# First weights of an encoder loaded and split by halves between x's chunks, and a final norm that multiplies from PSUM

## The chip, the core and the metric

The kernel runs on one core of a Trainium2 chip. The metric is the device time of one execution in microseconds; before and after are compared by the median of several runs. The core has five engines that work at the same time and wait for each other by semaphores: TensorE (PE) multiplies matrices, VectorE (DVE), ScalarE (ACT) and GpSimd (POOL) do elementwise work, and SyncE (SP) issues the transfers between HBM and the on-chip memory. [...]

## The reference, cut to what matters

Two layers of an encoder over 512 positions of width 1024, in fp32. The change touches the first projection and the last norm.

```python
for l in range(2):
    x = x + hybrid_mixer(rms_norm(x, norm_mix[l]), w_in[l], ...)   # neighbourhood and grouped-query attention
    x = x + memory_cross_attention(rms_norm(x, norm_mem_q[l]), ...)
    x = x + conv_ffn(rms_norm(x, norm_ffn[l]), w_up[l], ..., w_down[l])
return rms_norm(x, norm_final)

def rms_norm(x, g):
    return x * rsqrt(mean(x * x, axis=-1) + 1e-6) * g
```

The first thing that is multiplied is `rms_norm(x, norm_mix[0]) @ w_in[0]`, a product of 512x1024 by 1024x2304.

## The kernel before, in words

x is held transposed, as eight tiles `xT[0..7]` of 128 features (partitions) by 512 positions. To keep nearly fp32 accuracy at the speed of a shorter format, every operand is split into two parts, `hi` (rounded) and `lo` (the remainder), and a product is three matmuls: hi x hi, hi x lo, lo x hi (`mm3`, `gemm_T`). The gain of a norm is multiplied into x when x is split (`Norm.operand`: ScalarE makes hi with the gain as its scale, VectorE makes lo). The factor 1/rms isn't known yet at that time; it is multiplied into the result of the projection later. It comes from the squares of x (`Norm.square`), which are added up over the chunks, summed over the partitions by matmuls with a vector of ones (`Norm.stat`), raised to the power -0.5 on GpSimd, and spread over all partitions by matmuls (`Norm.spread`, `row_rep`), which end in a PSUM tile `tr`. ScalarE copies that tile to `rep` in SBUF, and later products read `rep`.

**The weights.** All weight tiles of the program stand in one list, `plan`, in order of use. `emit_raw` issues the load of the next entry on SP's queue; `emit_split` casts it to hi on ScalarE and subtracts on VectorE or GpSimd to get lo. A raw weight tile has two buffers (`N_RAW`), so that a load waits until the split before the last has freed its buffer; `eng` "x" takes the tile from another pool. Before the main program the kernel writes out its first loads by hand: a small piece of the parameters (the gains of the first norm), then `xT[0]`, the first weights (two halves of 256 KB), `xT[1]`, the second weights (512 KB in one transfer), `xT[2]`, `xT[3]`, the third weights (512 KB), `xT[4]` to `xT[7]`, all on SP's queue. A chunk of x is 256 KB too. The matching splits follow in the same order, on ScalarE in the order written (`ACT_IN_ORDER`); on VectorE they are left to the scheduler. Ten matmuls on an identity (`N_WARM`) run on TensorE while the first loads are on their way.

**The first projection** (`project_first`) multiplies three weight tiles (units 0, 1, 2) in an order by pieces, so that TensorE starts on the first chunks of x: chunks 0 and 1 of unit 0, of unit 1, then chunks 2 and 3 of both, chunks 0 to 3 of unit 2, and so on up to chunk 7; 72 matmuls of 128x128 by 128x512. The norm's statistic follows.

**The last stage** (`down_last`) computes the last part of the feed-forward block in two halves of 256 positions, eight rows of 128 features each. When a row is done, VectorE adds it to `xT`, and ScalarE squares it for the final norm. For rows 2 and 5 GpSimd then multiplies `xT` by the final gain `gfin` (`scale`). `finish` spreads 1/rms and makes the output: rows 2 and 5 as `xT * rep` on GpSimd, the others on VectorE as `(xT * gfin) * rep`, two inputs and a scalar in one instruction, all from SBUF. Four transfers per half carry it out, two rows each. The first half's `finish` runs in the middle of the second half's matmuls, the second half's stands at the very end of the program.

The order of a queue is that of the program where it says so (`InOrder`: TensorE, SP, and ScalarE at the start), and that of the tile scheduler elsewhere; `behind(n)` lowers the priority of what is written in it.

Of the kernel before, what the change touches and what calls it, by code (L numbers as in the profile page):

```python
# [11 lines left out]
F32R = mybir.dt.float32r  # L12
AF = mybir.ActivationFunctionType
# [5 lines left out]
P = 128  # L19
# [29 lines left out]
GQA_FILL = [2300] * 16 + [3000] * 4  # L49
MEM_FILL = [1, 1, 1, 2, 1, 0, 0, 2, 0, 1, 2]  # L50
MEM_STEPS = [0, 0, 1, 0, 1, 1, 1, 1, 1, 1, 1] + [0] * 9
W_BEHIND, N_RAW, N_W, AHEAD, AHEAD_HELD, N_WARM, N_LATE, N_FIRST = 45, 2, 4, 2, 5, 10, 4, 3


class InOrder:
# [117 lines left out]
def encoder_kernel(ctx: ExitStack, tc: tile.TileContext, t: dict, out: bass.AP):  # L173
# [58 lines left out]
    plan, raws, ready = [], [], []  # L232
    done = [0]

    def emit_raw():
        key, loads, nk, ncol, eng = plan[len(raws)]
        if eng[1:] == "x":
            raw = rtile((nk, ncol), F32)
        else:
            raw = wpool.tile([P, nk, ncol], F32, tag="raw", name=nm("raw"), bufs=N_RAW)  # L240
        for dst, src in loads:
            SP.dma_start(dst(raw), src)
        raws.append(raw)

    def emit_split(act=ACT, cuts=2):
        n = len(ready)
        key, loads, nk, ncol, eng = plan[n]
        raw = raws[n]
        raws[n] = None
        if key[0] in ("up", "down", "memq", "memo"):  # L250
            cuts = 1
        if eng[1:] == "r":
            hi, lo = rtile((nk, ncol)), rtile((nk, ncol))
        else:
            hi = wpool.tile([P, nk, ncol], F32R, tag="hi", name=nm("hi"))
            lo = wpool.tile([P, nk, ncol], F32R, tag="lo", name=nm("lo"))
        with behind(W_BEHIND if done[0] and key[0] not in ("up", "down") else 0):
            for i in range(cuts):
                k = slice(nk * i // cuts, nk * (i + 1) // cuts)
                act.copy(hi[:, k], raw[:, k])  # L260
                (POOL if eng[0] == "P" else DVE).tensor_sub(lo[:, k], raw[:, k], f(hi)[:, k])  # L261
        ready.append((hi, lo))

    def get_w(key, ahead=AHEAD):
        n = done[0]
        assert plan[n][0] == key, (plan[n][0], key)
        ahead = n + 1 + ahead
        while ahead < min(len(plan), n + 1 + AHEAD_HELD) and plan[ahead][4][1:] == "r":
            ahead += 1
        while len(ready) < min(len(plan), ahead):  # L270
            while len(raws) < min(len(plan), len(ready) + N_RAW):
                emit_raw()
            emit_split()
        while len(raws) < min(len(plan), len(ready) + N_RAW):
            emit_raw()
        done[0] += 1
        w = ready[n]
        ready[n] = None
        return w

    def cols(key, w, k0, nk, c0, ncol, eng="P"):
        src = w[k0 * P : (k0 + nk) * P, c0 : c0 + ncol].rearrange("(k p) c -> p k c", p=P)
        if plan:
            loads = [(lambda r: r, src)]
        else:
# [70 lines left out]
    ones = cpool.tile([P, 1], F32, name="ones")  # L356
    nc.vector.memset(ones, 1.0)
    ACT_IN_ORDER.copy(small(1), ones)
    SP.dma_start(par[:, 0, 0:8], t["par"][:, 0, 0:8])
    for c in range(KC):  # L360
        if c in (1, 2, 4):
            emit_raw()
        SP.dma_start(xT[c], t["xT"][c * P : (c + 1) * P, :])
    qkg = cpool.tile([P, DEPTH, 2], F32, name="qkg")
    gfin = cpool.tile([P, KC], F32, name="gfin")

# [25 lines left out]
    def row_rep(rstd, n, tag, bufs):  # L392

        pr = ps_t()
        for b in range(n):
            PE.matmul(pr[:, b * P : (b + 1) * P], rstd[:, b : b + 1].to_broadcast([P, P]), ident,
                      start=True, stop=True)
        rep = tpool.tile([P, n * P], F32, tag=tag, name=nm(tag), bufs=bufs)
        ACT.copy(rep, pr[:, : n * P])
        return rep  # L400

    class Norm:

# [12 lines left out]
            ACT.copy(xT[c], pm)  # L416
            self.square(c, src=pm)

        def operand(self, c, act=ACT, src=None):
# [3 lines left out]
            act.activation(hi, src, AF.Copy, scale=g)  # L423
            DVE.scalar_tensor_tensor(lo, src, g, f(hi), op0=ALU.mult, op1=ALU.subtract)

        def square(self, c, act=ACT, eng=None, src=None):
            sq = tmp((self.n,))
# [21 lines left out]
            self.rstd = rsqrt(pv[:, 0:nb], nb, 1.0 / D)  # L449

        def spread(self):
            self.rep = row_rep(self.rstd, self.n // P, "rep", 1)

    def split_psum(hi, lo, ps, scale=None):
        if scale is None:
# [100 lines left out]
    for l in range(DEPTH):  # L556
# [615 lines left out]
        def down_last(g):  # L1172

            j0, nj = GROUPS[g]
            ops = [acts.pop(j) for j in range(j0, j0 + nj)]
            ws = []

            def scale(half, m):
                xc = xT[m][:, 256 * half : 256 * half + 256]
                POOL.tensor_scalar(xc, xc, gfin[:, m : m + 1], 1.0, op0=ALU.mult, op1=ALU.mult)  # L1180

            def finish(norm):
                norm.spread()
                y = [rtile((4, 256), F32) for _ in range(2)]
                for k in range(KC):
                    yk, xk = y[k // 4][:, k % 4], xT[k][:, norm.cols]
                    if k in scaled:
                        POOL.tensor_mul(yk, xk, norm.rep)
                    else:
                        DVE.scalar_tensor_tensor(yk, xk, gfin[:, k : k + 1], norm.rep, op0=ALU.mult, op1=ALU.mult)  # L1190
# [4 lines left out]
            norms, scaled = [], (2, 5)  # L1195
            for half in range(2):
                cs = slice(256 * half, 256 * half + 256)
                hops = [(hi[:, cs], lo[:, cs]) for hi, lo in ops]
                norms.append(Norm(cols=cs))
                rows = []  # L1200
                for m in range(KC):
                    if half == 0:
                        ws.append(get_w(("down", g, m)))
                    rows.append(ps_mm()[:, :256])
                    late = half == 0 and m < N_LATE
                    gemm_T(rows[m], ws[m], hops, range(nj - 1 if late else nj), 0, nj - 1)
                    for i in [m] if not late else range(N_LATE) if m == N_LATE - 1 else []:
                        if late:
                            gemm_T(rows[i], ws[i], hops, [nj - 1], 0, nj - 1)
                        DVE.tensor_add(xT[i][:, cs], xT[i][:, cs], rows[i])  # L1210
# [106 lines left out]
```

## Time and profile before

| | us |
|---|---|
| median of 3 runs | 1401.05 |
| lowest, highest | 1397.9, 1404.61 |
| the profiled execution | 1401.19 |
| its span in the profile | 1399.2 |

In the rows of the profile, a time is in us from the start of the span unless ns is given. PE is TensorE's matmuls, PEld its weight loads. A row of the timeline gives start, length, engine, line of the kernel, operation, output and inputs with their shapes, and in brackets how long the engine was idle before and what ended that. A cast is the making of hi, `lo<-raw,hi` that of lo. A line L63 is the helper that keeps an engine in program order, L76 the one that issues matmuls, so such rows are told apart by their tiles. The chain of waits is followed back from the last instruction: it names at each time the piece of work on which the end depended.

### The profile page before, as it was taken

The numbers are of one execution on the slowest core, as the hardware profiler recorded it, in microseconds if no ns is written. First come the engines' busy times: TensorE is split into PE (matmuls) and PEld (weight loads), VectorE is DVE, ScalarE is ACT, GpSimd is POOL, SyncE is SP. The second block draws the span as 40 slices with busy tenths as digits, with TensorE's granted clock in tenths as the row PEclk, the third lists the DMA queues.
The fourth block names the chain that finished last, engine by engine and source line by source line (L and its number), as shares of the span: only waits on it lengthen the run. The fifth ranks groups of instructions, "written<-read, shape, count | busy, mean of one in ns | idle before, by whom it ended". The sixth has DMA issues, their size and how long they took to land.

```text
span 1399.2 us, 19213 instructions
## 1 busy us (share of the span) xinstructions
PE 1358.8 (97%) x7092; PEld 1158.8 (83%) x7092; DVE 835.1 (60%) x1421; ACT 702.8 (50%) x1308; POOL 722.9 (52%) x541
## 2 busy tenths in 40 slices
PE   9999899989999999999999989999999999999997
PEld 7897789878888888888888878897788888888897
DVE  5666766363687178358446557744638833861874
ACT  6676577655443144234556656765554423432441
POOL 2458776635544444444635677756264444444452
PEclk9999999999999999999999999999999999999998
DMA  7653312312333333332356523223133333333321
GB/s 210 181 149 95 89 46 71 111 61 61 94 102 103 93 91 96 100 102 84 118 148 167 135 65 95 70 70 103 46 90 102 95 94 102 89 92 106 100 82 60
DMA packets 218173, 138.83 MB, mean 99 GB/s; under 512 B 5984, under 2 KB 211040, under 8 KB 218080
## 3 DMA queue, kind: packets, MB, share of 16 engines
q1 hardware_dynamic: 218080, 137.60, 34.5%
q8 instruction: 56, 0.92, 0.3%
q14 instruction: 37, 0.30, 0.1%
HBM read 125.00 MB, written 2.10 MB: 91 GB/s over the span
## 4 chain that ended last, share of the span: by engine, by line
PE 88%; DVE 4%; ACT 3%; issue 2%; POOL 1%; DMA 1%; SPq 0%; DVEq 0%; ACTq 0%; POOLq 0%
PE mm L76 80%; PE sc L76 3%; PE tr L63 3%; PE tr L76 1%; ACT hi L260 1%; DVE r L457 1%; DMA raw<-in_w_down 1%; POOL lo L261 0%; POOL r L261 0%; DVE xg L457 0%; DMA raw<-in_w_in 0%; DVE s L859 0%; ACT t L800 0%; ACT t L799 0%; DVE t L801 0%
## 5 line engine op out<-in xcount | busy, mean ns | idle before, releaser
L261 POOL TENSOR_TENSOR lo<-raw,hi 128x1024 fp32r<-128x1024 f32 (+2 forms) x268 | 499.6, 1876 | 507.9 <-ACT hi L260 476.3
L76 PE MATMUL mm<-xg,hi 128*128 128x512 f32 x1984 | 617.7, 393 | 4.3 <-DVE t L801 2.9
L76 PEld LDWEIGHTS mm<-xg,hi 128*128 128x128 f32 x1984 | 369.9, 189 | 80.1 <-DVE t L801 3.3
L260 ACT CAST hi<-raw 128x512 fp32r<-128x512 f32 (+2 forms) x276 | 224.5, 836 | 347.0 <-PE mm L76 288.4
L76 PE MATMUL mm<-xg,lo 128*128 128x512 f32 x992 | 387.7, 391 | 0.0
L76 PE MATMUL mm<-r,hi 128*128 128x512 f32 (+1 forms) x1160 | 336.1, 374 | 2.5 <-DVE r L457 2.0
L76 PEld LDWEIGHTS mm<-r,hi 128*128 128x128 f32 x1160 | 210.3, 189 | 41.2 <-DVE r L457 2.8
L1141 DVE SCALAR_TENSOR_TENSOR t<-t,par,t 128x7 f32<-128x7 f32 (+1 forms) x352 | 201.9, 642 | 34.0 <-ACT t L1134 34.0
L76 PEld LDWEIGHTS mm<-xg,lo 128*128 128x128 f32 x992 | 187.1, 189 | 40.3 <-DVE lo L261 0.7
L76 PE MATMUL mm<-r,lo 128*128 128x512 f32 (+1 forms) x580 | 216.1, 373 | 0.0
L76 PEld LDWEIGHTS mm<-r,lo 128*128 128x128 f32 x580 | 109.3, 188 | 19.2
L1126 DVE TENSOR_TENSOR t<-mm,rep 128x512 f32<-128x512 f32 x88 | 60.2, 688 | 78.6 <-PE mm L76 62.1
L463 POOL TENSOR_SCALAR t<-t,s 128x512 f32<-128x512 f32 (+1 forms) x112 | 66.3, 607 | 75.2 <-DVE s L710 38.2
L1143 ACT ACTIVATE t<-t 128x512 f32<-128x512 f32 x44 | 27.9, 633 | 134.7 <-DVE t L1141 134.7
L1147 DVE TENSOR_TENSOR r<-t,r 128x512 fp32r<-128x512 f32 x44 | 90.5, 2056 | 7.3 <-ACT r L1146 4.3
L1170 DVE TENSOR_TENSOR xT<-xT,mm 128x512 f32<-128x512 f32 x32 | 21.9, 686 | 106.8 <-PE mm L76 106.8
L76 PE MATMUL sc<-r,r 128*128 128x256 f32 (+1 forms) x352 | 73.2, 339 | 4.4 <-DVE r L457 1.8
L63 PE MATMUL tr<-ident,t 128*128 128x128 f32 x456 | 62.8, 274 | 11.8 <-DVE r L457 3.8
L63 PEld LDWEIGHTS tr<-ident,t 128*128 128x128 f32 x456 | 52.4, 140 | 20.4 <-issue 7.9
L1134 ACT ACTIVATE t<-t,par 128x512 f32<-128x512 f32 x88 | 66.9, 807 | 3.3 <-DVE t L1126 3.3
L76 PE MATMUL mm<-r,r 128*128 128x256 f32 (+1 forms) x428 | 62.5, 297 | 0.1
L76 PEld LDWEIGHTS sc<-r,r 128*128 128x128 f32 x352 | 51.8, 191 | 10.6 <-ACT r L456 3.0
(134 smaller groups left out, 1538.9 us busy)
## 6 DMA issues: line engine op xcount, KB each, us to landing
raw<-in_w_up SPq DMA_DIRECT2D x88, 512.0 KB, 3.9
raw<-in_w_in SPq DMA_DIRECT2D x34, 512.0 KB, 4.7
raw<-in_w_down SPq DMA_DIRECT2D x32, 448.0 KB, 3.8
raw<-in_w_mem_kv SPq DMA_DIRECT2D x16, 512.0 KB, 4.1
raw<-in_w_down SPq DMA_DIRECT2D x16, 512.0 KB, 4.2
r<-in_bias SPq DMA_DIRECT2D x16, 384.0 KB, 5.9
r<-r SPq DMA_DIRECT2D x22, 256.0 KB, 5.5
raw<-in_w_out SPq DMA_DIRECT2D x8, 512.0 KB, 3.7
```

The source lines that it names most:

```text
L63: return lambda *a, **k: self.tc.keep_in_program_order(op(*a, **k))
L76: return self.tc.keep_in_program_order(self.engine.matmul(out, lhsT, rhs, **k))
L260: act.copy(hi[:, k], raw[:, k])
L261: (POOL if eng[0] == "P" else DVE).tensor_sub(lo[:, k], raw[:, k], f(hi)[:, k])
L457: DVE.tensor_sub(lo, ps, f(hi))
L463: eng.tensor_scalar(e, e, sums[:, col : col + 1], 1.0, op0=ALU.mult, op1=ALU.mult)
L1126: DVE.tensor_mul(u, us[side], ffn.rep)
L1134: ACT.activation(cc, u, AF.Identity, bias=par[:, l, CB + ch : CB + ch + 1], scale=w[1])
L1141: DVE.scalar_tensor_tensor(cc[:, dst], u[:, src], wi, cc[:, dst], op0=ALU.mult, op1=ALU.add)
L1143: ACT.activation(cs[0], cs[0], AF.Silu)
L1147: DVE.tensor_sub(acts[j][1], cs[0], f(acts[j][0]))
L1170: DVE.tensor_add(xT[m], xT[m], pm)
```

## The change

It has two parts.

1. **The start.** The first three weight tiles are each loaded in two halves of four chunks, 256 KB each, and the halves stand among the chunks of x in a list, `FIRST`: x0, first half of the weights 0 (`w00`), x1, `w10`, x2, x3, `w20`, x4, `w01`, x5, `w11`, `w21`, x6, x7. Loads and splits both follow it. The first parameters are issued on ScalarE's queue in place of SP's. The casts stay on ScalarE, but for that of `w00`, which goes to VectorE; VectorE's own work at the start is now in the order written as well (`DVE_IN_ORDER`), and stands as cast of `w00`, lo of x0, lo of `w00`, lo of x1, and so on. In `project_first` the first piece multiplies the four products with the first weights' hi ahead of the two with its lo. The warm-up has eight matmuls in place of ten.
2. **The end.** `scale` covers all eight rows and runs on ScalarE, with lowered priority, so that `xT` holds x times the final gain before 1/rms is known. The products of `finish` on VectorE become `xT * tr`: two inputs, of which the second is the spread norm where TensorE left it, in PSUM. GpSimd still makes rows 2 and 5 from the copy `rep`, which ScalarE still makes. In the built program VectorE's first product of a half waits for that copy.

```diff
-W_BEHIND, N_RAW, N_W, AHEAD, AHEAD_HELD, N_WARM, N_LATE, N_FIRST = 45, 2, 4, 2, 5, 10, 4, 3
+W_BEHIND, N_RAW, N_W, AHEAD, AHEAD_HELD, N_WARM, N_LATE, N_FIRST = 45, 2, 4, 2, 5, 8, 4, 3
...
     def cols(key, w, k0, nk, c0, ncol, eng="P"):
-        if plan:
+        if len(plan) >= 3:
             loads = [(lambda r: r, src)]
         else:
             h = nk // 2
...
-    SP.dma_start(par[:, 0, 0:8], t["par"][:, 0, 0:8])
-    for c in range(KC):
-        if c in (1, 2, 4):
-            emit_raw()
-        SP.dma_start(xT[c], t["xT"][c * P : (c + 1) * P, :])
+    FIRST = ["x0", "w00", "x1", "w10", "x2", "x3", "w20", "x4", "w01", "x5", "w11", "w21", "x6", "x7"]
+    nc.scalar.dma_start(par[:, 0, 0:8], t["par"][:, 0, 0:8])
+    first_loads = []
+    for n in FIRST:
+        c = int(n[1])
+        if n[0] == "x":
+            SP.dma_start(xT[c], t["xT"][c * P : (c + 1) * P, :])
+            continue
+        if c == len(first_loads):
+            first_loads.append(raw_tile())
+        raw, loads = first_loads[c]
+        dst, src = loads[int(n[2])]
+        SP.dma_start(dst(raw), src)
...
     nn = Norm(G_MIX, 0)
-    for c in range(KC):
-        nn.operand(c, ACT_IN_ORDER)
-        if c in (0, 1, 3):
-            emit_split(ACT_IN_ORDER)
+    DVE_IN_ORDER = InOrder(tc, nc.vector)
+    for n in FIRST:
+        c = int(n[1])
+        if n[0] == "x":
+            nn.operand(c, ACT_IN_ORDER, dve=DVE_IN_ORDER, hi_only=c == 0)
+            continue
...
+        raw, (hi, lo) = raws[c], ready[c]
+        k = slice(4 * int(n[2]), 4 * int(n[2]) + 4)
+        if n == "w00":
+            DVE_IN_ORDER.tensor_copy(hi[:, k], raw[:, k])
+            nn.operand(0, lo_only=True, dve=DVE_IN_ORDER)
+        else:
+            ACT_IN_ORDER.copy(hi[:, k], raw[:, k])
+        DVE_IN_ORDER.tensor_sub(lo[:, k], raw[:, k], f(hi)[:, k])
...
+                if (u, k0) == (0, 0):
+                    for k in range(2):
+                        PE.matmul(pms[u], w[u][0][:, k], xg[k][0], start=k == 0, stop=False)
+                        PE.matmul(pms[u], w[u][0][:, k], xg[k][1], start=False, stop=False)
+                    for k in range(2):
+                        PE.matmul(pms[u], w[u][1][:, k], xg[k][0], start=False, stop=False)
+                    continue
...
             def scale(half, m):
                 xc = xT[m][:, 256 * half : 256 * half + 256]
-                POOL.tensor_scalar(xc, xc, gfin[:, m : m + 1], 1.0, op0=ALU.mult, op1=ALU.mult)
+                with behind(20):
+                    ACT.activation(xc, xc, AF.Copy, scale=gfin[:, m : m + 1])
...
-                    if k in scaled:
+                    if k in (2, 5):
                         POOL.tensor_mul(yk, xk, norm.rep)
                     else:
-                        DVE.scalar_tensor_tensor(yk, xk, gfin[:, k : k + 1], norm.rep, op0=ALU.mult, op1=ALU.mult)
+                        DVE.tensor_mul(yk, xk, norm.psum)
...
-                        if i in scaled:
-                            scale(half, i)
+                        scale(half, i)
```

More of the change, by code (lines that the diff above doesn't have):

```diff
@@ L233, in encoder_kernel, with raw_tile @@
     done = [0]
-    def emit_raw():
+    def raw_tile():
         key, loads, nk, ncol, eng = plan[len(raws)]
@@ L240, in emit_raw @@
             raw = wpool.tile([P, nk, ncol], F32, tag="raw", name=nm("raw"), bufs=N_RAW)
+        raws.append(raw)
+        return raw, loads
+    def emit_raw():
+        raw, loads = raw_tile()
         for dst, src in loads:
             SP.dma_start(dst(raw), src)
-        raws.append(raw)
     def emit_split(act=ACT, cuts=2):
@@ L399, in row_rep @@
         ACT.copy(rep, pr[:, : n * P])
-        return rep
+        return rep, pr[:, : n * P]
     class Norm:
@@ L417, in close, with operand @@
             self.square(c, src=pm)
-        def operand(self, c, act=ACT, src=None):
+        def operand(self, c, act=ACT, src=None, dve=DVE, hi_only=False, lo_only=False):
             src = xT[c] if src is None else src
@@ L422, in operand @@
             hi, lo = self.ops[c]
-            act.activation(hi, src, AF.Copy, scale=g)
-            DVE.scalar_tensor_tensor(lo, src, g, f(hi), op0=ALU.mult, op1=ALU.subtract)
+            if not lo_only:
+                act.activation(hi, src, AF.Copy, scale=g)
+            if not hi_only:
+                dve.scalar_tensor_tensor(lo, src, g, f(hi), op0=ALU.mult, op1=ALU.subtract)
         def square(self, c, act=ACT, eng=None, src=None):
@@ L451, in spread @@
         def spread(self):
-            self.rep = row_rep(self.rstd, self.n // P, "rep", 1)
+            self.rep, self.psum = row_rep(self.rstd, self.n // P, "rep", 1)
     def split_psum(hi, lo, ps, scale=None):
@@ L547, in encoder_kernel @@
     nn = Norm(G_MIX, 0)
-    for c in range(KC):
-        nn.operand(c, ACT_IN_ORDER)
-        if c in (0, 1, 3):
-            emit_split(ACT_IN_ORDER)
+    DVE_IN_ORDER = InOrder(tc, nc.vector)
[4 more added lines that the diff above has]
+            continue
+        if c == len(ready):
+            if plan[c][4][1:] == "r":
+                ready.append((rtile((KC, P)), rtile((KC, P))))
+            else:
+                ready.append(tuple(wpool.tile([P, KC, P], F32R, tag=tag, name=nm(tag)) for tag in ("hi", "lo")))
+        raw, (hi, lo) = raws[c], ready[c]
[3 more added lines that the diff above has]
+            nn.operand(0, lo_only=True, dve=DVE_IN_ORDER)
+        else:
+            ACT_IN_ORDER.copy(hi[:, k], raw[:, k])
+        DVE_IN_ORDER.tensor_sub(lo[:, k], raw[:, k], f(hi)[:, k])
+        if n[2] == "1":
+            raws[c] = None
     for c in range(KC):
@@ L1193, in finish @@
                                  y[k // 4][:, k % 4 : k % 4 + 2])
-            norms, scaled = [], (2, 5)
+            norms = []
             for half in range(2):
```

## The prediction

> **What bounds the kernel now.** I read the page's head and its summary of the chain first, then the chain itself at the start and at the end, and last the timeline of each engine in those two places.
>
> ```profile
> span 1399.2 us, 19213 instructions
> PE 1358.8 (97%) x7092; PEld 1158.8 (83%) x7092; DVE 835.1 (60%) x1421; ACT 702.8 (50%) x1308; POOL 722.9 (52%) x541
> PE 88%; DVE 4%; ACT 3%; issue 2%; POOL 1%; DMA 1%; SPq 0%; DVEq 0%; ACTq 0%; POOLq 0%
> ```
>
> TensorE is busy for 97% of the span and carries 88% of the chain. The diff takes no product out of the sum but two warm-up matmuls; so it can only shorten what stands before the first unbroken run of matmuls and what stands behind the last one. The built program bears this out: between the loads and splits of the start and the final rows, the order on every engine is the same as before, apart from one reciprocal that swaps places with its neighbour. What is gained at the start is carried through 1,350 us as a shift, because the middle hangs on TensorE.
>
> The chain of waits at the start (start, length, what):
>
> ```profile
> 3.21 6.23 DMA raw<-in_w_in
> ...
> 9.47 0.63 ACT hi L63
> ...
> 10.14 17.02 PE mm L76 x66
> 27.16 0.79 PE tr L76 x8
> ```
>
> Until 10.14 the chain is a load: 512 KB of the second weights arrive in one piece, and the first cast of them frees TensorE. Then 66 of the 72 products of the first three projections run without a break up to 27.16, where the statistic of the norm follows. The timeline of TensorE and its windows (the eighth number, after POOL, is the granted clock):
>
> ```profile
> 1.35 4.63 PE L76 MATMUL tr<-ident 128*128 128x128 f32 x20 [1.35 <-POOL ident masks.py:199]
> ...
> 8.47 0.51 PE L76 MATMUL mm<-xg,hi 128*128 128x512 f32 x1 [0.97 <-ACT xg L63]
> 9.26 0.50 PE L76 MATMUL mm<-xg,hi 128*128 128x512 f32 x1 [0.28 <-DVE xg L424]
> ...
> 16.12 0.61 PE L76 MATMUL mm<-xg,hi 128*128 128x512 f32 x2
> 16.80 0.61 PE L76 MATMUL mm<-xg,hi 128*128 128x512 f32 x2
> ...
> 10.00:11.00 1.00, 0.86 (x3) 0.43 (x3) 0.88 (x2) 1.00 (x3) 0.00 (x0) 0.82 1.20 309
> 13.00:14.00 1.00, 1.00 (x3) 0.74 (x3) 0.73 (x2) 1.00 (x3) 0.00 (x0) 0.50 1.05 377
> 14.00:15.00 1.00, 1.00 (x6) 0.80 (x5) 1.00 (x2) 1.00 (x3) 0.00 (x0) 0.97 1.11 325
> ```
>
> Three products take 0.68 us at the full clock (16.12 to 16.80), 0.227 each. After the gaps of 0.97 and 0.28 the clock falls to a half at about 10.64 (0.82 over that microsecond) and is back at about 14.03, 3.4 us later. In those 3.4 us 7.5 products pass in place of 15: the half clock costs 7.5 x 0.227 = 1.7 us.
>
> **The start, step by step.** When loads land is read from ScalarE, which takes them in order and idles for them:
>
> ```profile
> 0.72 0.40 SPq L63 DMA_DIRECT2D par<-in_par  x1
> ...
> 4.53 0.72 ACT L63 ACTIVATE xg<-xT,par 128x512 fp32r<-128x512 f32 x1 [2.33 <-DMA xT<-in_xT]
> 6.98 0.62 ACT L63 CAST hi<-raw 128x512 fp32r<-128x512 f32 x1 [1.06 <-DMA raw<-in_w_in]
> 9.47 1.14 ACT L63 CAST hi<-raw 128x512 fp32r<-128x512 f32 x2 [1.05 <-DMA raw<-in_w_in]
> 12.62 1.14 ACT L63 CAST hi<-r 128x512 fp32r<-128x512 f32 x2 [0.78 <-DMA r<-in_w_in]
> ...
> 5.28 0.75 DVE L424 SCALAR_TENSOR_TENSOR xg<-xT,par,xg 128x512 fp32r<-128x512 f32 x1 [4.19 <-ACT xg L63]
> 5.96 0.69 DVE L261 TENSOR_TENSOR lo<-raw,hi 128x512 fp32r<-128x512 f32 x1
> ```
>
> In units of 256 KB, the 1st, 3rd, 6th and 10th unit land at 4.5, 6.96, 9.45 and 12.6: 0.80 us a unit from the third on. The bytes are the same after the change, so is the rate; only the order differs. The parameter load leaves SP's queue and saves it the 0.46 us to its next issue. ScalarE issues it before its table load, 2.33 us of idleness ahead of the first use: free. So unit n lands at 6.5 + 0.80 (n - 3), the first at 4.07.
>
> In the new order x1 is unit 3 (6.5), the first half of the second weights unit 4 (7.3), where 1.5 MB had to land before. VectorE's copy of the first half weights has no row; from below it is the 0.358 us of a 256-wide one-input operation (the row stands at the end of this part), from above the 0.69 of the two-input one; I take 0.5. With unit 2 a step of 0.80 behind the first, at 4.9: copy to 5.4, lo of x0 to 6.15, lo of the weights to 6.85, lo of x1 from 7.2 (ScalarE's hi of x1 takes 0.72 from 6.5) to 7.95, lo of the second weights to 8.65. VectorE takes these in a fixed order, so each blocks those behind it, and the last to release TensorE is x1's lo: the fourth product starts at 7.95. Two lo products and then 66 others have their operands in time: chunk 2 has its lo at 9.55 and is wanted at 10.0, chunk 3 at 10.35 for 10.9, and the last chunk's lo at 16.7 is wanted at 19.5 or later.
>
> So an unbroken run of 69 products begins at 7.95 in place of 66 at 10.14. At the full clock it needs 69 x 0.227 + 0.35 (the last one's drain) = 16.0, to 24.0; with one spell of half clock 1.65 more, to 25.6. In the new order TensorE is fed thinly from 5.05 (eight warm-ups of the ten, 3.7 us) to 7.95, six products' worth or less in 2.9 us, as before from 5.98 to 10.14; I take one half-clock spell again. **Start: 27.16 - 25.6 = 1.55 us gained.**
>
> Next in line is the statistic, which needs all squares added:
>
> ```profile
> 17.17 1.12 ACT L260 CAST hi<-raw 128x512 fp32r<-128x512 f32 x2
> 18.87 5.73 DVE L439 TENSOR_TENSOR t<-t,t 128x512 f32<-128x512 f32 x6 [0.87 <-ACT t L63]
> ...
> raw<-in_w_in SPq DMA_DIRECT2D x1, 512.0 KB, 7.5
> ...
> L463 DVE TENSOR_SCALAR t<-t,s 128x256 f32<-128x256 f32 x32 | 10.1, 358 | 0.4
> ```
>
> The sum is ready at 24.6. It trails the cast of the fourth weights (17.17) by 7.4 us, since six of the squares stand behind that cast on ScalarE and GpSimd's split of it slows VectorE's adds. The load of the fourth weights (third row: 7.5 us from issue to landing, issued at 9.65) reuses the first weights' buffer, and that is now free only after the first weights' second half, unit 9 in the order, is split: at 12.65 instead of 8.3. It is unit 15 and 16 of the line either way, lands at about 16.9, and the statistic stays ready at 24.6 or before, ahead of 25.6. This caps the gain at 27.16 - 24.6 - 0.15 = 2.4 us whatever the clock does.
>
> [...]
>
> **The end, step by step.** The chain from the last copy, SP's first output issue, and the output loads:
>
> ```profile
> 1391.44 0.38 ACT rep L399
> 1391.84 1.05 DVE r L1190
> 1392.89 0.86 DVEq L1312
> 1393.76 1.58 DVE r L1190 x4
> ...
> 1391.89 1.59 POOL L1188 TENSOR_TENSOR r<-xT,rep 128x256 f32<-128x256 f32 x2 [1.84 <-ACT rep L399]
> 1393.78 0.37 SPq L63 DMA_DIRECT2D out<-r  x1
> out<-r SPq DMA_DIRECT2D x8, 256.0 KB, 2.4
> ```
>
> While GpSimd runs its two products, VectorE's first two take 1.05 and 0.86 us; the four after that take 0.395 each. The first output leaves when both are done, at 1393.78. After the change VectorE's second operand is in PSUM. What that is worth under GpSimd, four rows show:
>
> ```profile
> 1353.86 2.13 POOL L261 TENSOR_TENSOR r<-raw,r 128x896 fp32r<-128x896 f32 x1 [2.12 <-ACT r L260]
> 1356.52 2.13 POOL L261 TENSOR_TENSOR r<-raw,r 128x896 fp32r<-128x896 f32 x1 [0.54 <-ACT r L260]
> 1354.26 1.50 DVE L1210 TENSOR_TENSOR xT<-xT,mm 128x256 f32<-128x256 f32 x4 [0.60 <-PE mm L76]
> 1357.10 1.83 DVE L436 TENSOR_TENSOR t<-t,t 128x256 f32<-128x256 f32 x1 [1.35 <-ACT t L428]
> ```
>
> Inside GpSimd's first split four adds with one operand in PSUM take 1.50 us, 0.375 each; inside the second one add with both operands in SBUF takes 1.83. So the products become 0.41 each: the first two end at 1392.66 in place of 1393.75, the sixth at 1394.3 in place of 1395.34. The outputs follow 1.0 us earlier. They start no sooner than before: in the built program the first product still waits for ScalarE's copy (0.38), since both read the same PSUM tile. **End: 1.0 us gained.**
>
> [...]
>
> The price is 16 scalings by the gain on ScalarE. In the second half they stand in gaps and the last is done well before the copy at 1391.44. In the first half four fall ahead of a cast that TensorE needs:
>
> ```profile
> 1356.35 1.34 ACT L428 ACTIVATE t<-xT 128x256 f32<-128x256 f32 x4
> 1359.98 0.94 ACT L260 CAST r<-raw 128x896 fp32r<-128x896 f32 x1 [2.29 <-DMA raw<-in_w_down]
> L716 ACT ACTIVATE t<-t,s 128x256 f32<-128x256 f32 x16 | 8.3, 517 | 0.8 <-DVE s L710 0.7
> ```
>
> At 0.517 each they end at 1357.69 + 2.07 = 1359.76, 0.2 us before the load lands. Free, but only just; each microsecond over that would be paid in full. GpSimd's four scalings fall away, off the path.
>
> **Sum.** The profiled execution took 1401.19 us, next to the median of 1401.05. 1401.19 - 1.55 - 1.0 = 1398.6.
>
> **The rivals.** *The clock stays full*: for it, the thin stretch shrinks from 4.2 to 2.9 us, shorter than one spell; against, before fell after gaps of under 1 us. The statistic then ends the stage: 2.4 + 1.0 off, 1397.8. *VectorE stays slowed by GpSimd at the end*: x still comes from SBUF; against, the four adds above. The end gains 0.1: 1399.5. *The fourth weights come late*, the one on the slower side: their issue waits in SP's queue for VectorE's ninth split. If a unit costs 1.0 us in the new order, between the 0.80 of the later rows and the 1.23 of the first two steps (4.5 to 6.96), the ninth lands at 12.5 and that split ends at 13.8; if the load then still takes its 7.5 us, it lands at 21.3 and the statistic starts at 28.85. The start loses 1.7, the end gains 1.0: 1401.9. It decides from a landing of 19.6 on (from there the start gains nothing), and slower in all from 20.6. Against: most of the 7.5 us was queueing behind bytes that by 13.8 have gone.
>
> **How the numbers follow.** Forecast 0.5, full clock 0.25, slowed products 0.12, late weights 0.08, anything else 0.05. The first three span 1397.8 to 1399.5. The three runs of before lie from 1397.9 to 1404.6, so a median can stand some 2.5 us to either side: 1395.3 to 1402.0, which takes in the fourth. A measurement of this kernel can tell about 0.5%, 7.0 us, from no change. No case reaches 1394.0 by its sum; the runs' spread and the rest carry 0.09 across it, and 0.03 over 1408.1. Within: 0.88.
>
> **What would show it.** Right: the unbroken run of products starts near 8.0 and the statistic near 25.6; the fourth weights' cast is at 17; the final products take 0.41 and the first output is issued 0.85 us after VectorE's first product starts. Wrong: a stall of TensorE before the statistic, a gap on it behind the cast near 1360, or a change in the middle of the kernel, which nothing here foresees.

## The result, and the profile after

| | before | after |
|---|---|---|
| median, us | 1401.69 (12 runs) | 1397.97 (12 runs) |
| lowest, highest | 1397.9, 1404.61 | 1395.88, 1399.36 |
| ratio to before, 95% interval | | 0.9975, 0.9964 to 0.9986 |
| the profiled execution, its span | 1401.19, 1399.2 | 1398.05, 1396.3 |

The kernel became faster by 0.25%. 1398.6 was forecast, with a range of 1395.3 to 1402.0 and "within 0.5%" as the likely answer; all three hold.

The head of the page of the kernel after:

```profile
span 1396.3 us, 19216 instructions
PE 1357.5 (97%) x7088; PEld 1158.8 (83%) x7088; DVE 832.4 (60%) x1422; ACT 710.3 (51%) x1323; POOL 719.2 (52%) x537
```

TensorE bounds the kernel as it did, with four matmuls fewer in the trace. ScalarE has the sixteen added scalings (702.8 to 710.3 us), and nothing in the total says where the time came from. The places do. First TensorE's timeline at the start, then its windows there (the eighth number is the granted clock):

```profile
7.15 0.49 PE L76 MATMUL mm<-xg,hi 128*128 128x512 f32 x1 [0.96 <-ACT xg L63]
7.94 0.80 PE L76 MATMUL mm<-xg,hi 128*128 128x512 f32 x1 [0.29 <-DVE xg L63]
8.53 1.05 PE L76 MATMUL mm<-xg,lo 128*128 128x512 f32 x2
...
25.21 0.95 PE L76 MATMUL tr<-ones,t 128*128 128x1 f32 x8
```

```profile
8.00:9.00 1.00, 1.00 (x3) 0.81 (x4) 0.91 (x2) 1.00 (x2) 0.00 (x0) 0.50 1.10 352
...
11.00:12.00 1.00, 1.00 (x5) 0.78 (x4) 1.00 (x2) 0.86 (x2) 0.00 (x0) 0.91 1.18 305
```

The products run without a break from 7.94 (10.14 before), with one stretch of half clock, and the statistic stands at 25.21 (27.00 in the same view of before). So far the prediction's own figures: 7.95, one stretch, 25.6. But the next rows of the chain, from 24 to 40 us, name something that the prediction never mentions:

```profile
23.94 1.30 DVE lo L265 x2
25.26 4.04 DMA raw<-in_w_in
29.40 1.14 ACT hi L264 x2
...
31.06 0.71 DVE mm L649
...
34.54 4.60 PE mm L76 x24
```

The chain runs past the statistic. VectorE's split ends, which frees a raw buffer; the load into that buffer (the seventh weights) lands 4 us later; ScalarE casts it; and behind that cast stands ScalarE's copy of the spread norm, which all evictions wait for. ScalarE's own timeline there, after and then before:

```profile
29.40 1.14 ACT L264 CAST hi<-raw 128x512 fp32r<-128x512 f32 x2 [4.03 <-DMA raw<-in_w_in]
30.45 0.58 ACT L412 COPY rep<-tr 128x512 f32<-128x512 f32 x1
```

```profile
30.42 1.14 ACT L260 CAST hi<-raw 128x512 fp32r<-128x512 f32 x2 [3.67 <-DMA raw<-in_w_in]
31.76 0.59 ACT L399 COPY rep<-tr 128x512 f32<-128x512 f32 x1 [0.20 <-PE tr L76]
```

Before, the copy waited 0.20 us for TensorE; after, it follows the cast without a gap and waits for nothing but its turn. Of 1.79 us gained at the statistic the copy got 1.31.

At the end, VectorE's timeline, ScalarE's last copy, and SP's output issue. `mm` and `tr` are tiles in PSUM, the on-chip memory that TensorE's matmuls write; in the profiles of before and after VectorE and ScalarE read such tiles, as in these rows (0.42 and 0.37 us for 128x256), and no row of GpSimd does.

```profile
1386.19 0.42 DVE L1251 TENSOR_TENSOR xT<-xT,mm 128x256 f32<-128x256 f32 x1 [1.19 <-PE mm L76]
...
1390.18 2.07 DVE L1231 TENSOR_TENSOR r<-xT,tr 128x256 f32<-128x256 f32 x6 [2.04 <-ACT rep L412]
```

```profile
1389.78 0.37 ACT L412 COPY rep<-tr 128x256 f32<-128x256 f32 x1 [2.17 <-PE tr L76]
```

```profile
1390.96 1.98 SPq L63 DMA_DIRECT2D out<-r  x4
```

The six products take 2.07 us (3.49 before), and the first output is issued 0.78 us after the first product starts (1.94 before). From the last row's add to the end of the span it is 1396.3 - 1386.19 = 10.11 us.

### The profile page after: what moved, and what is told of

The parts are those of the page before. It is cut to its first block, busy times and chain, and to the rows that moved or that the text cites. A ratio compares the mean times of both kernels' runs of the same rounds, so it can differ in the third digit from the quotient of the medians.

```text
span 1396.3 us, 19216 instructions
## 1 busy us (share of the span) xinstructions
PE 1357.5 (97%) x7088; PEld 1158.8 (83%) x7088; DVE 832.4 (60%) x1422; ACT 710.3 (51%) x1323; POOL 719.2 (52%) x537
## 4 chain that ended last, share of the span: by engine, by line
PE 88%; DVE 4%; ACT 4%; issue 2%; DMA 1%; POOL 1%; SPq 0%; DVEq 0%; ACTq 0%
PE mm L76 80%; PE sc L76 3%; PE tr L63 3%; PE tr L76 1%; DMA raw<-in_w_in 1%; ACT hi L264 1%; DVE r L472 1%; ACT t L744 1%; POOL lo L265 0%; DMA xT<-in_xT 0%; ACT t L840 0%; DVE t L841 0%; DVE s L899 0%; ACT t L839 0%; DVE xg L472 0%
```

## The experiments

Each is an edit of the kernel after, unless said otherwise. The kernel before has a median of 1401.6 to 1402.0 in the comparisons below (29 to 34 runs each).

**The start alone: `e1_start_only`.** The end is as before.

```diff
-                    ACT.activation(xc, xc, AF.Copy, scale=gfin[:, m : m + 1])
+                POOL.tensor_scalar(xc, xc, gfin[:, m : m + 1], 1.0, op0=ALU.mult, op1=ALU.mult)
...
-                        DVE.tensor_mul(yk, xk, norm.psum)
+                        DVE.scalar_tensor_tensor(yk, xk, gfin[:, k : k + 1], norm.rep, op0=ALU.mult, op1=ALU.mult)
```

> The change's start with the end of before. Theory (two independent gains): the first matmul run starts near 7.9 and the norm's statistic near 25.2 as after the whole change, ScalarE's copy of the spread norm near 30.5 in place of 31.8, and the last products are as before: the first two take about 1.0 and 0.9 us, the first output leaves about 1.9 us after the first product starts. The time falls by about 1.3 us from before, what reaches that copy. Rival (the clock decides): the gain at the statistic is there in the profile, but the number of half-clock spells, 1.7 us each, differs from run to run, so that the median is as before within 1 us, or lower by 3 us or more.

1399.65 us, ratio 0.998 (0.9969 to 0.9991). The copy of the first spread norm starts at 30.53, and from the last add to the end of the span it is 11.33 us. The group of the final products:

```profile
L1230 DVE SCALAR_TENSOR_TENSOR r<-xT,gfin,rep x12: 471/474/1048, 1376.7 to 1393.5; 128x256 f32<-128x256 f32 x12
```

Most take 0.474 us, and those beside GpSimd up to 1.05; the first output is issued 1.94 us after the first product. The places came out as expected; the time fell by 2.0 where 1.3 was expected, which the interval allows.

**The end alone: `e2_end_only`.** The kernel before, with the end of the kernel after (the same lines the other way round).

> The start of before with the change's end. Theory: the statistic at the start is near 27.0 as before; the final products take about 0.41 each, the first output leaves 0.8 us after the first product starts in place of 1.9, and the span ends about 7.0 us after the last row's add in place of 8.0 at the same clock. The time falls by 1.0 to 1.3 us. Rival (the scalings on ScalarE delay the last weights' casts): TensorE waits behind the cast near 1360 longer than the 0.29 us of before, and the time falls by under 0.5 us.

1400.03 us, ratio 0.9989 (0.9975 to 1.0004). In place the end came as expected: the first output is issued 0.78 us after the first product. The 8.0 and 7.0 us of the expectation are not the whole stretch: from the last add to the end of the span it is 10.23 here and 11.96 before. By the medians the start alone gives 2.0, the end alone 1.6, both 3.7: the parts add up, but each has an interval of some 1.5 to 2 us to either side, and that of the end alone takes in no change.

**The products from SBUF: `e3_sbuf_products`.**

```diff
-                        DVE.tensor_mul(yk, xk, norm.psum)
+                        DVE.tensor_mul(yk, xk, norm.rep)
```

> The changed kernel, but VectorE's final products read the copy of the spread norm in SBUF; the scaling by the gain stays on ScalarE and the products stay plain two-input ones. Theory (PSUM as the second operand keeps VectorE out of GpSimd's way): the first products are slow again while GpSimd runs its two, 0.7 us or more each for the first two, and the first output leaves 1.5 us or more after the first product starts; 0.7 to 1.1 us of the end's gain are gone. Rival (taking the gain's scalar out of the product is what made it short): the products stay at about 0.41 each and nothing is lost.

1398.76 us, ratio 0.9975 (0.9965 to 0.9986). The group of the products with the operand in SBUF, then that of the kernel after:

```profile
L1231 DVE TENSOR_TENSOR r<-xT,rep x12: 410/420/966, 1376.3 to 1392.7; 128x256 f32<-128x256 f32 x12
```

```profile
L1231 DVE TENSOR_TENSOR r<-xT,tr x12: 411/414/420, 1376.5 to 1391.8; 128x256 f32<-128x256 f32 x12
```

Three numbers in such a row are the shortest, the median and the longest. The medians agree, 420 and 414 ns: an operand in PSUM costs nothing here. The longest do not: 966 against 420. Beside GpSimd a product with both operands in SBUF takes up to 966 ns, more than twice its time (the second and the third of the last half), and one with an operand in PSUM at most 420. The first output is issued 1.32 us after the first product, where 1.5 or more was expected, and the stretch from the last add to the end is 10.78, longer by 0.67. So the rival holds in part: of the 1.22 us between `e1_start_only` (11.33) and the kernel after (10.11), the operand in PSUM is worth 0.67; the other 0.55 is there with both operands in SBUF, when the products have lost their scalar. On the whole time this is within the spread.

**No copy, all products on VectorE: `e4_no_copy`.**

```diff
-                    if k in (2, 5):
-                        POOL.tensor_mul(yk, xk, norm.rep)
-                    else:
-                        DVE.tensor_mul(yk, xk, norm.psum)
+                    DVE.tensor_mul(yk, xk, norm.psum)
...
+        if n == 2:
+            return None, pr[:, : n * P]
```

> The changed kernel without ScalarE's copy of the spread norm at the end and without GpSimd's two products: all eight products of a half are VectorE's, from PSUM. Theory (the first product waited only for the copy): the first product starts about 0.42 us earlier after the spread, the first output leaves 0.4 us earlier, the eight products end 2.7 us after the first starts, the last output leaves at about the same time, and the span ends 0.3 to 0.4 us earlier, since the outputs are a stream of 0.75 us each behind the first. Rival (the last product sets the end): no gain, or 0.2 us lost.

1397.01 us, ratio 0.9967 (0.9956 to 0.9979), the lowest median of all; from the last add to the end 9.61, 0.50 less than after. Its start, which it shares with the kernel after, was more instructive. In its profiled execution the clock stayed full at the start (1.00 in its record from 6.63 us, through the place where it falls at 7.77 after), and TensorE shows:

```profile
23.85 1.05 PE L76 MATMUL tr<-ones,t 128*128 128x1 f32 x8 [0.39 <-DVE t L456]
...
28.44 1.16 PE L76 MATMUL tr<-ident,s 128*128 128x128 f32 x8 [0.67 <-POOL s L402]
```

The statistic came 1.36 us earlier than in the kernel after and waited for the squares' sum; the spread then waited for GpSimd's power; and ScalarE's copy stood at 30.21 all the same, against 30.45. The gain of a full clock was gone by the copy.

**TensorE's gaps at the start filled: `e5_filled`.**

```diff
-... N_WARM, N_LATE, N_FIRST = 45, 2, 4, 2, 5, 8, 4, 3
+... N_WARM, N_LATE, N_FIRST = 45, 2, 4, 2, 5, 9, 4, 3
...
                         PE.matmul(pms[u], w[u][0][:, k], xg[k][0], start=k == 0, stop=False)
+                        for _ in range(k):
+                            PE.matmul(warm[:, 0:P], ident, ident, start=True, stop=True)
                         PE.matmul(pms[u], w[u][0][:, k], xg[k][1], start=False, stop=False)
+                        for _ in range(2 - 2 * k):
+                            PE.matmul(warm[:, 0:P], ident, ident, start=True, stop=True)
```

> The kernel after, with TensorE's gaps at the start filled by matmuls on the identity: one more warm-up, two behind the second product, one behind the third. Theory one (the rest of the start's gain was lost on ScalarE, whose cast of the seventh weights waits for a load): no stretch of half clock between 8 and 12 us, the statistic at 23.6 to 24.2, held by the squares' sum and not by TensorE, but the copy of the spread norm still ends its wait at 30.2 to 30.5, and the time is that of the kernel after within 0.5 us, but for stretches of half clock elsewhere. Theory two (the clock at the start sets the gain): the copy comes 1.5 us earlier as well, near 29.0, and so does all behind it, about 1396.5 in place of 1398.0.

The place came out as theory one has it: no half clock at 8, the statistic at 24.06, the copy at 30.48. (The copy is weak evidence here: half clock from 25.08 to 28.50, where two hi products took 1.05 us in place of 0.62, held the spread until 29.4, and the copy followed it as closely as it followed the cast.) The time did not: 1400.7 us, ratio 0.9983 (0.9968 to 0.9998; 8 runs, 1396.55 to 1405.46). Its profiled execution was a long one (span 1403.7), and what it lost it lost between 115 and 149 us and between 780 and 802 us, far from the edit.

**The copy ahead of the cast: `e6_rep_first`.**

```diff
+        if n == 6:
+            act = ACT_IN_ORDER
...
-        ACT.copy(rep, pr[:, : n * P])
+        (ACT_IN_ORDER if early else ACT).copy(rep, pr[:, : n * P])
```

> The kernel after, with ScalarE's copy of the first spread norm put ahead of its cast of the seventh weights, and the cast behind the next work in line. Theory one (the copy is late because it stands behind a cast that waits for a load): the copy starts where TensorE's spread ends, near 29.6 in place of 30.55, the gap on TensorE before 34.5 us shortens from 1.85 to about 1.0, and 0.8 us come off the whole; if the shorter gap brings no stretch of half clock near 36 us, up to 2.5. Rival (the seventh weights are themselves wanted early): the cast moved behind stalls TensorE later by as much, and the time stays.

1401.13 us, ratio 0.9988 (0.9974 to 1.0002; 1395.36 to 1405.03): no gain. In the profiled execution the copy came no earlier, at 30.94, and GpSimd's timeline shows a second piece in line:

```profile
25.05 2.99 POOL L267 TENSOR_TENSOR lo<-raw,hi 128x512 fp32r<-128x512 f32 x2 [4.33 <-ACT hi L266]
27.99 1.03 POOL L404 TENSOR_TENSOR s<-s,mhalf 128x4 f32<-128x4 f32 x1
```

The power of the statistic (second row) stands behind a split of 3 us; the spread came at 29.48, into a stretch of half clock.

**Two PSUM tiles for the last norm: `e8_two_tiles`.**

```diff
+        src = pr
+        if n == 2:
+            src = ps_t()
+            for b in range(n):
+                PE.matmul(src[:, b * P : (b + 1) * P], rstd[:, b : b + 1].to_broadcast([P, P]), ident, start=True, stop=True)
-        ACT.copy(rep, pr[:, : n * P])
+        ACT.copy(rep, src[:, : n * P])
```

> The kernel after, with the final norm spread twice, into two tiles: VectorE's products read the first, ScalarE's copy for GpSimd reads the second. If the copy stands in the path of the end only because both read one tile, VectorE's first product starts about 0.4 us earlier after the spread, the first output goes 0.4 earlier, and the stretch from the last row's add to the end of the span falls from 10.1 to about 9.7. Rival (GpSimd's two products, which now start later by the second spread, end last): the stretch stays at 10.1 or grows by the 0.3 to 0.4 us of the second spread.

1398.62 us, ratio 0.997 (0.9959 to 0.9982). VectorE's first product came 4.04 us after the last add (3.99 after), GpSimd's products at 1392.13, 1.35 us behind VectorE's, and the stretch to the end grew to 10.66, as the rival has it. But this profile can't decide: the eight spread matmuls took 2.08 us, at half clock (eight of the same form take 1.05 at full clock, at 28.88 in the kernel after), while the four of the kernel after took 0.71 at full clock. By an estimate from these, 1.05 in place of 2.08 takes most of the growth away.

**Halves, but in the old order: `e9_old_order`.**

```diff
-    FIRST = ["x0", "w00", "x1", "w10", "x2", "x3", "w20", "x4", "w01", "x5", "w11", "w21", "x6", "x7"]
+    FIRST = ["x0", "w00", "w01", "x1", "w10", "w11", "x2", "x3", "w20", "w21", "x4", "x5", "x6", "x7"]
```

> The kernel after, with both halves of each of the first three weights side by side at the places that the whole weights had before (x0, w00, w01, x1, w10, w11, x2, x3, w20, w21, x4 to x7); the parameters on ScalarE's queue, VectorE's order and the first products' order as in the kernel after. If the order by halves is what brought the start forward: the unbroken run of products starts at 9.2 to 9.6 in place of 7.94 and the statistic comes near 26.3 with one stretch of half clock. Rival (the other edits of the start did it): the run starts near 8 and the statistic at 25.2. The whole time follows by no more than 1.3 us either way, since the copy of the spread norm stands near 30.5 in both as long as the statistic is in time for it; with the statistic at 26.3 the copy comes near 31.1.

1397.47 us, ratio 0.9974 (0.9964 to 0.9984). The run starts at 8.62, between the two guesses, the statistic follows at 26.00 (17.38 us later, where it is 17.27 after, with its one stretch of half clock), and the copy at 30.77, where it waits for TensorE's spread again. So the order by halves brings the statistic 0.8 us forward and the copy 0.3; the other edits of the start (transfers of 256 KB in place of 512, the parameters' queue, VectorE's order), which weren't taken apart, bring the copy the other 1.0 of the 1.31. Each of these rests on one profile, and the time does not show the order by halves at all: 1397.47 is no slower than the kernel after (1397.97 above, 1397.43 below).

**Everything next in line moved: `e12_chain`.** The edits of `e5_filled` and `e6_rep_first`, and the split that stood ahead of the power goes to VectorE.

```diff
-                (POOL if eng[0] == "P" else DVE).tensor_sub(lo[:, k], raw[:, k], f(hi)[:, k])
+                (POOL if eng[0] == "P" and n != 5 else DVE).tensor_sub(lo[:, k], raw[:, k], f(hi)[:, k])
```

> The kernel after with the three things next in line behind the first statistic moved at once: TensorE's gaps at the start filled by identity matmuls (statistic at 24.0 in place of 25.2), the split of the sixth weights taken from GpSimd, where it stood ahead of the power, to VectorE (power at 26.7 in place of 27.6), and ScalarE's copy put ahead of its cast of the seventh weights. If these three are what held the start's gain back: the power starts near 26.7, the spread near 27.9, the copy at 28.8 to 29.4 in place of 30.45, and the median is 1.0 to 1.6 us under that of the kernel after. Rival (what follows hangs on the middle's own waits and stretches of half clock, or on the seventh weights, now cast late): the copy comes earlier but the median does not move, or rises.

TensorE, and ScalarE's copies of the spread norms:

```profile
23.81 1.05 PE L76 MATMUL tr<-ones,t 128*128 128x1 f32 x8 [0.23 <-DVE t L456]
...
27.54 1.05 PE L76 MATMUL tr<-ident,s 128*128 128x128 f32 x8
```

```profile
28.62 0.59 ACT L63 COPY rep<-tr 128x512 f32<-128x512 f32 x1 [3.77 <-PE tr L76]
...
285.70 0.59 ACT L414 COPY rep<-tr 128x512 f32<-128x512 f32 x1 [2.41 <-PE tr L76]
...
971.24 0.59 ACT L414 COPY rep<-tr 128x512 f32<-128x512 f32 x1 [2.41 <-PE tr L76]
```

The copy comes 1.83 us earlier than after: those three pieces were what held it. And yet 1399.06 us, ratio 0.9977 (0.9966 to 0.9989): no faster than the kernel after, as the rival has it.

**The same with the end of `e4_no_copy`: `e13_best`.**

> The kernel of the run before it in this list, with the end that had all eight final products on VectorE and no copy: by the sum 1.0 to 1.6 us from the start and 0.5 to 1.0 from the end under the kernel after, near 1396; if the start's rearrangement brings nothing, 1397, as the end alone measured.

1399.12 us, ratio 0.9984 (0.9971 to 0.9996), the copy at 28.67. The forecast of 1396 to 1397 fails.

**The kernel after once more: `e14_after_again`.**

> The kernel after once more, beside the other two and on the same chip, to tell its own spread: a median within 1 us of 1397.97 if the runs are comparable from call to call, and a profile whose copy of the first spread norm stands at 30.2 to 30.6 whatever the stretches of half clock at the start do, if the cast ahead of it holds it.

1397.43 us, ratio 0.9969 (0.9957 to 0.998). Its copies of the spread norms:

```profile
30.45 0.58 ACT L412 COPY rep<-tr 128x512 f32<-128x512 f32 x1
...
285.91 0.59 ACT L412 COPY rep<-tr 128x512 f32<-128x512 f32 x1 [2.41 <-PE tr L76]
...
968.91 0.59 ACT L412 COPY rep<-tr 128x512 f32<-128x512 f32 x1 [2.41 <-PE tr L76]
```

The statistic came at 24.55 here, 0.66 before that of the first profile, and the copy at the same 30.45. The lead of `e12_chain`, 1.83 at the first copy, is 0.21 at the second, and at the fifth `e12_chain` lies 2.33 behind.

**Where such a lead goes.** Between 115 and 165 us (the first layer's neighbourhood attention) TensorE stands idle some five times, for 0.6 to 1.9 us. Its rows behind the longer of those gaps, before, in `e14_after_again` and in `e12_chain`:

```profile
121.11 0.73 PE L76 MATMUL mm<-xg,hi 128*128 128x512 f32 x2 [1.44 <-DVE t L801]
126.05 0.66 PE L63 MATMUL tr<-ident,t 128*128 128x128 f32 x4 [0.63 <-DVE s L811]
140.46 0.63 PE L63 MATMUL tr<-ident,t 128*128 128x128 f32 x4 [1.90 <-DVE r L457]
150.66 1.05 PE L76 MATMUL tr<-pairs,t 128*128 128x2 f32 x8 [1.33 <-ACT t L800]
164.00 0.63 PE L63 MATMUL tr<-ident,t 128*128 128x128 f32 x4 [1.65 <-POOL r L508]
```

```profile
119.79 0.73 PE L76 MATMUL mm<-xg,hi 128*128 128x512 f32 x2 [1.44 <-DVE t L841]
138.36 0.63 PE L63 MATMUL tr<-ident,t 128*128 128x128 f32 x4 [1.91 <-DVE r L472]
148.57 1.05 PE L76 MATMUL tr<-pairs,t 128*128 128x2 f32 x8 [1.33 <-ACT t L840]
163.43 0.63 PE L63 MATMUL tr<-ident,t 128*128 128x128 f32 x4 [1.67 <-POOL r L523]
```

```profile
118.55 0.73 PE L76 MATMUL mm<-xg,hi 128*128 128x512 f32 x2 [1.44 <-DVE t L847]
123.71 0.66 PE L63 MATMUL tr<-ident,t 128*128 128x128 f32 x4 [0.86 <-DVE s L857]
138.11 0.63 PE L63 MATMUL tr<-ident,t 128*128 128x128 f32 x4 [1.91 <-DVE r L474]
149.91 1.05 PE L76 MATMUL tr<-pairs,t 128*128 128x2 f32 x8 [1.33 <-ACT t L846]
163.23 0.63 PE L63 MATMUL tr<-ident,t 128*128 128x128 f32 x4 [1.64 <-POOL r L525]
```

Two things differ. The gap at 126.05 and 123.71, where TensorE waits for VectorE, is there before and in `e12_chain`, and not in `e14_after_again`. The lead of `e12_chain` over `e14_after_again` is 1.24 us at the first of these rows and 0.25 at the row of 138.11: most of it is gone before any half clock, 1.0 of it at that gap. What makes VectorE late there is open.

The four other gaps are the same in all three, but the work between them is not equally fast. From the row with the gap of 1.9 us to the next it takes 10.20 and 10.21 us, and 11.80 in `e12_chain`; from there to the last row 13.34 before and 13.32 in `e12_chain`, and 14.86 in `e14_after_again`. The windows of `e12_chain` give the reason for the 11.80:

```profile
136.00:140.00 4.00, 2.09 (x11) 1.69 (x10) 3.12 (x5) 2.76 (x7) 1.45 (x2) 0.91 0.29 66
140.00:144.00 4.00, 4.00 (x18) 3.29 (x18) 1.56 (x4) 0.43 (x1) 2.56 (x2) 0.66 0.00 0
```

Behind one gap or another the clock falls to a half, and that costs 1.5 to 1.6 us; which gap it is changes from one execution to the next. (For `e14_after_again` the distance alone tells it; in the profile after, where the same distance is 14.83, the record has the fall at 151.13.) The two records of before and after show a pattern in it: in each the clock changes only at times that lie whole multiples of 3.413 us apart. Before, it falls at 10.64, 826.43 and 840.08 us (239 and 4 steps between them), after at 7.77, 35.08, 151.13 and 826.97 (8, 34 and 198 steps), and each of these falls lasts one step. The steps lie elsewhere in the two executions. Why one gap costs and another of the same length does not, no run shows. The second layer's attention, from 780 to 850 us, does the same: before, the falls at 826.43 and 840.08 come behind gaps of 1.91 and 1.33 us; after, there is one behind the gap of 1.91 and none behind that of 1.33. Between these places, the distance from one kernel to another at the same instruction stays within 0.2 us for hundreds of microseconds: that part of the middle does carry a shift.

## Why the prediction was right, and where not

- **The loads and the unbroken run: right.** 7.94 measured, 7.95 forecast; the fourth weights' cast at 16.59 for 17. The rival of late weights is out: their load was issued at 12.42 (forecast 12.65) and had landed when that cast began, 4.2 us later, not 7.5.
- **The half clock at the start: came, but as a toss.** The profile after shows it, and so does `e1_start_only`; four other executions with the same start (`e3`, `e4`, `e6`, `e8`) show none at that place. In `e1_start_only` and `e4_no_copy` the first four products start within 0.03 us of each other (4.97, 5.54, 6.71, 7.49 and 4.94, 5.51, 6.70, 7.48), and the clock falls in the first alone, at 7.81; in the second its record has full clock from 6.63 on. `e14_after_again` is a third case: its trace has no record of the clock before 10.58, and its two lo products from 7.75 on take 1.05 us as in the profile after, not 0.64 as in `e4_no_copy`, so it ran at half clock there. That the profile had the one stretch of the sum is luck. It began behind a gap of 0.96 us and within one of 0.29, in a thin stretch of 2.81 us (5.13 to 7.94): that this is shorter than one stretch of half clock (3.41 us), the reason given for the rival of a full clock, did not keep it full.
- **"Next in line is the statistic": the step that failed.** The squares' sum does cap the statistic (at 23.85, forecast 24.6). But a gain at the statistic isn't yet one of the kernel. Behind it stand GpSimd's power, held by a split until 27.3 to 28, and ScalarE's copy, held by a cast whose load lands at 29.4 (`e12_chain`, which moves all of this, has the copy 1.83 earlier). The kernel after gains 1.31 at the copy where 1.55 was forecast. The rival "the clock stays full", 1397.8, had its condition met in four profiles without the 0.8 us that it promised: in the three of them that leave ScalarE's order as it is, the copy stands at 30.36, 30.21 and 30.44, at most 0.24 earlier.
- **The end: right in mechanism, a little under in size.** The operand in PSUM takes VectorE out of GpSimd's way (`e3_sbuf_products`: at most 420 ns a product, against up to 966), so the rival of slowed products is out; but that is worth 0.67 of the gain below; the rest, 0.55, goes with the scalar taken out of the products (a median of 474 ns with it, 420 without), for which the sum has no term. The term was 1.0: the last add to the end of the span took 11.33 us in `e1_start_only`, 10.11 after, 1.22 less. Against before's own profile (1399.2 - 1387.24 = 11.96) it is 1.85; there the spread matmuls took 1.22 us at half clock, after 0.71 at full clock, as in `e1_start_only`; no run shows that the change does this.
- **ScalarE's scalings: free, as forecast.** The cast that four of them precede waits for its load still, 0.58 us:

```profile
1357.45 0.90 ACT L1221 ACTIVATE xT<-xT,gfin 128x256 f32<-128x256 f32 x2
1358.92 0.94 ACT L264 CAST r<-raw 128x896 fp32r<-128x896 f32 x1 [0.58 <-DMA raw<-in_w_down]
```

- **"Carried through 1,350 us as a shift": wrong.** Before's copies of the second and fifth spread norms, then those of the profile after:

```profile
286.45 0.59 ACT L399 COPY rep<-tr 128x512 f32<-128x512 f32 x1 [2.41 <-PE tr L76]
...
970.74 0.59 ACT L399 COPY rep<-tr 128x512 f32<-128x512 f32 x1 [2.41 <-PE tr L76]
```

```profile
286.87 0.59 ACT L412 COPY rep<-tr 128x512 f32<-128x512 f32 x1 [2.41 <-PE tr L76]
...
969.81 0.59 ACT L412 COPY rep<-tr 128x512 f32<-128x512 f32 x1 [2.41 <-PE tr L76]
```

The lead of 1.31 at the first copy was a lag of 0.42 by the second and a lead of 0.93 by the fifth. The two profiled executions agree with the sum (3.14 us apart, 2.55 forecast) partly by luck; what carries the verdict is the medians.

**What stays open.** The medians put the change at 3.7 us (2.0 to 5.0), and at 4.6 (2.8 to 6.0) in the second set, somewhat more than the 2.55 of the places. Part of that is the clock. The record has the mean granted clock of each run, to three decimals: it averages 0.9929 over the 94 runs of before in the comparisons above, and 0.9943 and 0.9947 over the two sets of the kernel after. By an estimate from these numbers, 0.0014 to 0.0018 of 1397 us, that is worth 2.0 to 2.5 us, or less where TensorE is not busy all through a stretch of half clock; with so few runs it is a rough figure. What is left, 1.7 to 2.1 us or more, is near the sum. The runs of the kernel after also scatter less (standard deviations 1.1 and 1.4 us, against about 2 of before). Whether the change itself makes the stretches of half clock fewer is open.

Half clock is not why `e12_chain` and `e13_best`, with a lead of 1.8 us at the copy, end no earlier: over their runs the mean granted clock is 0.9950 and 0.9949, no lower than after. So the lead goes in other waits. For `e12_chain` the gap at 123.71 shows 1.0 us of that in one profile; the rest, and the cause, are open. `e4_no_copy` beats the kernel before; that it beats the kernel after, 1397.01 against 1397.97 and 1397.43, can't be told from these runs.

## What to carry to other kernels

When a term of the sum ends at "then X is ready", follow X's reader on its own engine: what stands ahead of it in that queue, and what load releases that? Give the last of several products an operand in PSUM where GpSimd works beside VectorE (here at most 0.42 us a product, against up to 0.97 with both in SBUF). And where a stage has short gaps before TensorE, expect the clock to move the result for each stretch of half clock (here by 1.5 to 1.6 us, behind gaps of 1.33 and 1.91 us), either way: a gain of 1 to 2 us is shown by medians and by the place, never by two spans.

## What the runs showed of the hardware that had not been expected

- In the profiles of before and after the granted clock falls to a half seven times ahead of the end, each time for 3.413 us and 0.5 to 2.3 us behind a gap of 0.96 to 1.91 us on TensorE; behind other gaps of the same length in the same place it does not. In each of the two it changes only at whole multiples of 3.413 us. The stretch before the fall need not be idle: in the profile after, three products start between 4.36 and 7.77, where it falls.
- Beside two GpSimd products of the same size, a VectorE product of two SBUF operands took up to 0.97 us in place of 0.42; with one operand in PSUM at most 0.420. GpSimd's own pair took 1.41 us beside the PSUM products and 1.82 beside the SBUF ones.
